# Edges of the stages in a Strassen-Winograd encoder block: five pairs begun among the token sums, separate buffers for the last down products, branch weights loaded during attention

## The chip, the cores and the metric

One core of a Trainium2 chip runs the whole block in one launch. The metric is device time in microseconds (us), the median of three runs: 2261.47 for the kernel before (2260.64 to 2265.18).

The core has a matrix engine (TensorE, PE in the rows), three elementwise engines (VectorE or DVE, ScalarE or ACT, GpSimd or POOL), and SyncE (SP), whose queue issues nearly all DMAs here. Each engine takes its instructions in the order in which they were written.

## The reference

One layer on a float32 array of 1024 tokens by 1024 features:

```python
x = x + 0.5 * swiglu(rmsnorm(x), w_gate1, w_up1, w_down1)     # FFN_DIM 2816
p = rmsnorm(x) @ w_in            # columns for attention, mLSTM and two gates
A = mla(p)                       # 8 heads, low-rank q and kv, rotary key
B = mlstm(p)                     # 4 heads, forward and backward scans
x = x + (sigmoid(g_a) * (A @ w_branch_a) + sigmoid(g_b) * (B @ w_branch_b)) @ w_out
x = x + 0.5 * swiglu(rmsnorm(x), w_gate2, w_up2, w_down2)
out = rmsnorm(x)

def swiglu(x, w_gate, w_up, w_down):
    return (jax.nn.silu(x @ w_gate) * (x @ w_up)) @ w_down
```

## The kernel before

**Numbers.** Every float32 operand of a matmul is split into a high and a low part, `H = copy to the short format` on ScalarE and `L = x - H` on VectorE. A matmul of two operands is three: HH, HL, LH. A weight quarter is split in `split_quarter` (L249 on ScalarE, L250 on VectorE), its twelve matmuls are `product` (L255 to L257), all of them from 128 rows by 512 columns.

**The large products.** Both FFNs and the output projection use a Strassen-Winograd scheme: seven products of half-size matrices stand for eight. It needs sums of quarters of the left matrix, of the right one and of the results. `combine_x` builds those of the tokens: for tiles 0 to 3 of 128 tokens it transposes, splits (L362, L363) and keeps a copy of two quarters (`kept`, copied at L369 by ScalarE); for tiles 4 to 7 it forms the sums T1 to T4 from these copies. VectorE makes most other sums (`vsum` L262, `into` L266).

**Gate and up (`gate_up`).** Column pairs j = 0 to 10, each with a gate half and an up half, each of seven products; 14 products per pair. Products 1 and 2 need only the tokens of tiles 0 to 3, so a pair can be *begun* early: `begin(j)` computes them, writes product 1 to DRAM (`f1p`) and one finished quarter to `f1h`. Pairs 0, 1 and 2 are begun, `begin(0)` before the tokens 4 to 7 are combined and the other two behind them; such a pair has ten products left in the main loop `pairs()`. The loop's step k issues product k, then prepares product k + 4 (`prep`: a sum if it needs one, ScalarE's high part, VectorE's low part right behind it), then takes in the result of product k - 1 (`post`), then one of the leftover sums of an earlier pair. `in_order` ties the engines to that order. Results go to DRAM (`f1h`, `f2h`), as do sums of the down weights (`f1w`, `f2w`). `four` in `sums_left` overwrites the tile that `two` has just stored to DRAM.

**Down (`down`).** Seven products in the order 1, 6, 2, 5, 7, 3, 4. Each runs over 11 steps j, each with two loads (L579, L580), ScalarE's high part (L582), VectorE's low part (L583) and 12 matmuls (L590). The loads take their buffers from `ring`: eight in turn, four of the pool `rw`, two with the tag `raw`, two with the tag `xn`. Where product 3 ends, the tokens 0 to 3 are final: `done` stores them and normalises them (RMS norm: L106 on ScalarE, L112 on VectorE, or L109 and L110 on GpSimd for tokens 1, 3 and 5) into tiles of the tags `xn` and `raw`, and product 4 follows, with transposes of the normalised tokens (L128) among it. In FFN1 `load_small` loads the narrow columns of `w_in` there in four pieces, again into `raw`, and splits them (L714 on ScalarE, L715 on GpSimd).

**Branch stage.** After attention, `branch_cols` loads (L1281) and splits the branch weights by column pairs; gates come from DRAM (`sg`, L1293), pass a sigmoid (L1294) and multiply the products (L1302).

Of the kernel before, what the change touches and what calls it, by code (L numbers as in the profile page):

```python
# [20 lines left out]
P = 128  # L21
# [30 lines left out]
def block_kernel(ctx, tc, a, out):  # L52
# [131 lines left out]
    QS = [P, 4, P]  # L184
# [60 lines left out]
    def split_quarter(R, src):  # L245
# [4 lines left out]
        nc.vector.tensor_tensor(out=L_, in0=src, in1=f32(H_), op=ALU.subtract)  # L250
        return H_, L_
# [17 lines left out]
    class Combined:  # L269


        def __init__(self, name, n):
            self.left = {m: [dram.tile([P, 512], F32, name=f"{name}h{m}_{j}") for j in range(n)] for m in range(1, 8)}
            self.right = {m: [dram.tile([P, 512], F32, name=f"{name}w{m}_{j}") for j in range(n)] for m in range(4, 8)}
            self.p1 = {(j, i): dram.tile([P, 512], F32, name=f"{name}p{j}_{i}") for j in range(min(n, 3)) for i in range(2)}
# [5 lines left out]
        def sums_left(self, R, j, c11, c12, c21, c22):  # L281
# [18 lines left out]
            def four():  # L300
                self.store(3, j, into(nc.vector, got[2], c21, got[2], ALU.subtract))
# [47 lines left out]
    def combine_x(R, t, xn, X, kept):  # L349
# [42 lines left out]
    AHEAD = 4  # L392

    def gate_up(R, X, wg, wu, wd, comb, hooks={}):
# [41 lines left out]
        def products_of(j, i, h):  # L436

            v = {}
# [9 lines left out]

            def prep1():
                v["w"] = {1: split_quarter(R, raws[j, i][0])}  # L450

            def prep6():
# [3 lines left out]
                v["w"] = {**v.get("w", {}), 6: split_quarter(R, v["s2"])}  # L456

            def prep2():
                v["w"][2] = split_quarter(R, raws[j, i][1])

            def prep5():
                v["w"][5] = split_quarter(R, v["s1"])

            def prep7():
                v["s3"] = vsum(R, raws[j, i][0], raws[j, i][2], ALU.subtract)
                v["w"][7] = split_quarter(R, v["s3"])

            def prep3():
                s4 = into(nc.vector, v["s2"], raws[j, i][1], v["s2"], ALU.subtract)
                v["w"][3] = split_quarter(R, s4)  # L470

            def prep4():
                v["w"][4] = split_quarter(R, raws[j, i][3])
                if i == 0 and j + 1 < n:
                    raws[j + 1, 1] = load(wu, j + 1)
                elif i == 1 and j + 1 < n:
                    ld, tails[j + 1] = comb.sums_right(wd, j + 1, R.ring)
                    ld()
                    if j + 2 < n:
                        raws[j + 2, 0] = load(wg, j + 2)  # L480

            def mm(m, bank, B, start=True):
                def f():
# [5 lines left out]
                    product(v[bank], v["w"].pop(m), X[B], start, True)  # L489
# [30 lines left out]
        def pairs():  # L520
# [8 lines left out]
            def prologue():  # L529
# [6 lines left out]
                for it in items[:AHEAD]:  # L536
                    it[1]()
# [9 lines left out]
            def step(k):  # L547
# [10 lines left out]
                del rest[:1]  # L558
            for k in range(len(items)):
# [12 lines left out]
    def down(R, comb, resid, scale, xo, done, between=lambda: None, last=3):  # L572
# [3 lines left out]
        def products(m, banks, start, stop, tails=1):  # L576
            def load(j):
                r = R.ring(2)
# [34 lines left out]

        for t in range(NT):
            nc.sync.dma_start(out=xo[t], in_=resid[t * P:(t + 1) * P, :])
        a = [R.bank(0) for _ in range(4)]
        run(1, a, True, True)
# [25 lines left out]
        run(3, c, False, True, each=c12, tails=last)  # L643
# [6 lines left out]
        run(4, e, True, True, each=c21, step=step, tails=last)  # L650
# [56 lines left out]
    def load_small(pool):  # L707
        for k in range(0, KT, 2):
            raw = raw_tile()[:, :2 * NSM].rearrange("p (k f) -> p k f", k=2)
            rows = w_in[k * P:(k + 2) * P, :].rearrange("(k p) f -> p k f", p=P)  # L710
            nc.sync.dma_start(out=raw[:, :, 0:O_M], in_=rows[:, :, 0:O_M])
            nc.sync.dma_start(out=raw[:, :, O_M:NSM], in_=rows[:, :, O_G:O_G + 16])
            wH, wL = [pool.tile([P, 2, NSM], F32R, name="ws" + n, tag=f"ws{n}{k}") for n in "HL"]
            nc.scalar.activation(out=wH, in_=raw, func=AF.Copy)  # L714
# [662 lines left out]
```

## Time and profile before

| | us |
|---|---|
| median of three runs | 2261.47 (2260.64 to 2265.18) |
| the profiled execution | 2262.68, span 2260.9 |
| TensorE busy | 2125.0 (94%) |
| VectorE busy | 1513.8 (67%) |
| ScalarE busy | 964.8 (43%) |
| GpSimd busy | 358.5 (16%) |

The mean granted clock of TensorE is 0.974 of full speed. Times of the profile are counted from the start of the span. FFN1 takes the first 720 us or so, attention ends near 1386, FFN2 begins near 1580. A duration that the profile gives for a matmul includes its way through the engine; matmuls follow each other faster than that. A row of waits says which instruction of an engine stood idle and which instruction of another released it.

### The profile page before, as it was taken

The numbers are of one execution on the slowest core, as the hardware profiler recorded it, in microseconds if no ns is written. First come the engines' busy times: TensorE is split into PE (matmuls) and PEld (weight loads), VectorE is DVE, ScalarE is ACT, GpSimd is POOL, SyncE is SP. The second block draws the span as 40 slices with busy tenths as digits, with TensorE's granted clock in tenths as the row PEclk, the third lists the DMA queues.
The fourth block names the chain that finished last, engine by engine and source line by source line (L and its number), as shares of the span: only waits on it lengthen the run. The fifth ranks groups of instructions, "written<-read, shape, count | busy, mean of one in ns | idle before, by whom it ended". The sixth has DMA issues, their size and how long they took to land.

```text
span 2260.9 us, 27801 instructions
## 1 busy us (share of the span) xinstructions
PE 2125.0 (94%) x10091; PEld 1770.4 (78%) x10091; DVE 1513.8 (67%) x2201; ACT 964.8 (43%) x1509; POOL 358.5 (16%) x307
## 2 busy tenths in 40 slices
PE   6989999999977999999999998988999999999996
PEld 4777888888856888778888887867777888888885
DVE  6777777755464666466658886567877777765564
ACT  6323333333433433544358884235623333334433
POOL 1000000000021655233445442002100000000000
PEclk9999999999988999999999999999999999999998
DMA  7554444476643433222441004875555444566643
GB/s 199 193 200 159 163 159 163 163 272 191 194 154 110 131 109 118 88 84 85 149 145 48 29 1 152 302 245 187 190 196 191 141 164 151 183 210 231 195 159 140
DMA packets 238233, 358.41 MB, mean 159 GB/s; under 512 B 23696, under 2 KB 124944, under 8 KB 238096
## 3 DMA queue, kind: packets, MB, share of 16 engines
q1 hardware_dynamic: 232912, 346.16, 46.6%
q10 hardware_dynamic: 4608, 8.39, 1.0%
q8 instruction: 79, 1.29, 0.2%
q0 software_dynamic: 576, 2.10, 0.2%
q14 instruction: 58, 0.48, 0.1%
HBM read 246.94 MB, written 109.64 MB: 158 GB/s over the span
## 4 chain that ended last, share of the span: by engine, by line
PE 73%; DVE 11%; DMA 7%; ACT 4%; issue 3%; POOL 2%; SPq 0%; DVEq 0%; ACTq 0%; POOLq 0%
PE pb L590 19%; PE pb L255 10%; PE pb L257 10%; PE pb L256 10%; PE pin L85 3%; PE pin L83 3%; PE pin L84 3%; DVE s L266 2%; PE pP L1221 2%; DMA sg<-gb_d 2%; DVE s L262 1%; PE pav L1229 1%; PE pSc L83 1%; PE pav L1230 1%; DVE w L250 1%
## 5 line engine op out<-in xcount | busy, mean ns | idle before, releaser
L590 PE MATMUL pb<-w 128*128 128x512 f32 x2184 | 505.3, 394 | 33.8 <-ACT w L582 30.4
L590 PEld LDWEIGHTS pb<-w 128*128 128x128 f32 x2184 | 414.1, 190 | 124.5 <-ACT w L582 31.9
L583 DVE TENSOR_TENSOR w<-rw,w 128x1024 fp32r<-128x1024 f32 x182 | 221.7, 1223 | 213.8 <-ACT w L582 213.8
L582 ACT ACTIVATE w<-rw 128x1024 fp32r<-128x1024 f32 x182 | 192.8, 1062 | 299.2 <-PE pb L590 269.6
L249 ACT ACTIVATE w<-s 128x512 fp32r<-128x512 f32 x176 | 109.8, 630 | 339.2 <-DVE s L262 220.9
L93 POOL TENSOR_TENSOR rs<-ms,mhalf 128x1 f32<-128x1 f32 (+3 forms) x52 | 59.8, 1151 | 971.2 <-DVE ms L98 965.0
L250 DVE TENSOR_TENSOR w<-s,w 128x512 fp32r<-128x512 f32 x176 | 121.5, 691 | 109.0 <-ACT w L249 108.8
L255 PE MATMUL pb<-XH,w 128*128 128x512 f32 x352 | 143.0, 407 | 17.3 <-ACT s L407 10.4
L83 PE MATMUL pin<-HH,dH 128*128 128x512 f32 x384 | 152.3, 397 | 0.2 <-DVE TL L1197 0.2
L85 PE MATMUL pin<-HH,dL 128*128 128x512 f32 x384 | 150.8, 394 | 0.2 <-POOL dL L159 0.2
L84 PE MATMUL pin<-HL,dH 128*128 128x512 f32 x384 | 150.9, 393 | 0.0
L255 PE MATMUL pb<-YH,w 128*128 128x512 f32 x352 | 139.6, 398 | 11.7 <-ACT s L407 7.9
L257 PE MATMUL pb<-XH,w 128*128 128x512 f32 x352 | 141.1, 401 | 2.3 <-DVE w L250 2.3
L256 PE MATMUL pb<-XL,w 128*128 128x512 f32 x352 | 141.0, 400 | 0.0
L257 PE MATMUL pb<-YH,w 128*128 128x512 f32 x352 | 138.5, 393 | 0.2 <-DVE w L250 0.2
L256 PE MATMUL pb<-YL,w 128*128 128x512 f32 x352 | 138.4, 393 | 0.0
L250 DVE TENSOR_TENSOR w<-rw,w 128x512 fp32r<-128x512 f32 x148 | 103.8, 705 | 35.6 <-ACT w L249 35.1
L249 ACT ACTIVATE w<-rw 128x512 fp32r<-128x512 f32 x148 | 91.5, 626 | 45.0 <-ACT w L249 16.0
L266 DVE TENSOR_TENSOR s<-pb,s 128x512 f32<-128x512 f32 x152 | 103.4, 685 | 7.4 <-DMA s<-f1p 2.8
L255 PEld LDWEIGHTS pb<-XH,w 128*128 128x128 f32 x352 | 68.5, 195 | 34.8 <-ACT s L407 13.0
L411 ACT ACTIVATE h<-s 128x512 f32<-128x512 f32 x66 | 41.8, 633 | 120.4 <-DVE s L266 120.4
L1001 POOL MEMSET onesg<- 64x128 f32 x1 | 0.2, 198 | 585.1 <-DVE x L612 585.1
(322 smaller groups left out, 4697.8 us busy)
## 6 DMA issues: line engine op xcount, KB each, us to landing
rw<-in_ffn_w_gate SPq DMA_DIRECT2D x50, 512.0 KB, 5.7
rw<-in_ffn_w_up SPq DMA_DIRECT2D x50, 512.0 KB, 5.1
rw<-in_ffn_w_down SPq DMA_DIRECT2D x44, 512.0 KB, 3.7
rw<-f1h SPq DMA_DIRECT2D x77, 256.0 KB, 2.7
rw<-f2h SPq DMA_DIRECT2D x77, 256.0 KB, 2.8
rw<-in_ffn_w_down SPq DMA_DIRECT2D x66, 256.0 KB, 3.0
raw<-in_w_in SPq DMA_DIRECT2D x24, 512.0 KB, 4.0
f1h<-h SPq DMA_DIRECT2D x44, 256.0 KB, 2.1
```

The source lines that it names most:

```text
L83: nc.tensor.matmul(ps, wH, mH, start=start, stop=False)
L84: nc.tensor.matmul(ps, wH, mL, start=False, stop=False)
L85: nc.tensor.matmul(ps, wL, mH, start=False, stop=stop)
L249: nc.scalar.activation(out=H_, in_=src, func=AF.Copy)
L250: nc.vector.tensor_tensor(out=L_, in0=src, in1=f32(H_), op=ALU.subtract)
L255: nc.tensor.matmul(ps, w[0][:, k, :], B[0][:, k, :], start=start and k == 0, stop=False, skip_group_check=True)
L256: nc.tensor.matmul(ps, w[0][:, k, :], B[1][:, k, :], start=False, stop=False, skip_group_check=True)
L257: nc.tensor.matmul(ps, w[1][:, k, :], B[0][:, k, :], start=False, stop=stop and k == 3, skip_group_check=True)
L266: eng.tensor_tensor(out=out, in0=a, in1=b, op=op)
L582: nc.scalar.activation(out=H_, in_=r, func=AF.Copy)
L583: nc.vector.tensor_tensor(out=L_, in0=r, in1=f32(H_), op=ALU.subtract)
L590: nc.tensor.matmul(banks[t], l[:, 0, ts_], r[:, 1, :], start=start and j == 0 and i == 0, stop=stop and j == n - 1 and i == 2, skip_group_ ...
```

## The change

- **Begun pairs.** Five pairs are begun instead of three, and `begin` now stands between the combined tokens 4 to 7.
- **Kept copies.** The copies of the two token quarters are made by GpSimd, by adding H and L, instead of by ScalarE from PSUM.
- **Order in the loop.** Step k takes in the result of product k - 1 before it prepares product k + 4, and the low part of the prepared weight stands behind the leftover sum. `four` writes into another tile.
- **Down products 3 and 4** take their load buffers from the pool `rw` alone. The loads of `x` stand behind product 1.
- **Narrow columns of `w_in`** are loaded in one piece into a tile of their own before `down` starts; their low parts move from GpSimd to VectorE. A second token tile of narrow products is computed early.
- **Branch weights** of the first column pair are loaded at step 50 of attention.

```diff
-    QS = [P, 4, P]
+    AHEAD = 4
+    BEGUN = 5
...
-                self.store(3, j, into(nc.vector, got[2], c21, got[2], ALU.subtract))
+                self.store(3, j, into(nc.vector, c21, c21, got[2], ALU.subtract))
...
-            for n, v, s in zip(("B11", "B21"), ps, kept[i]):
+            for n, v in zip(("B11", "B21"), ps):
                 put(X[n], v)
-                nc.scalar.activation(out=s, in_=v, func=AF.Copy)
+            for n, s in zip(("B11", "B21"), kept[i]):
+                nc.gpsimd.tensor_tensor(out=s, in0=f32(X[n][0][:, :, c]), in1=f32(X[n][1][:, :, c]), op=ALU.add)
...
                 mm()
-                if k + AHEAD < len(items):
-                    items[k + AHEAD][1]()
                 if k:
                     after(k - 1)
+                low = items[k + AHEAD][1]() if k + AHEAD < len(items) else None
                 for f in rest[:1]:
                     f()
                 del rest[:1]
+                if low is not None:
+                    low()
...
-        def products(m, banks, start, stop, tails=1):
+        def products(m, banks, start, stop, tails=1, raw=R.ring):
             def load(j):
-                r = R.ring(2)
+                r = raw(2)
...
-        run(3, c, False, True, each=c12, tails=last)
+        run(3, c, False, True, each=c12, tails=last, raw=R.raw)
...
-        run(4, e, True, True, each=c21, step=step, tails=last)
+        run(4, e, True, True, each=c21, step=step, tails=last, raw=R.raw)
...
-    def load_small(pool):
+    def load_small():
+        raw = big.tile([P, KT, 512], F32, name="wsr", tag="big2")[:, :, 0:NSM]
...
-            nc.gpsimd.tensor_tensor(out=wL, in0=raw, in1=f32(wH), op=ALU.subtract)
+            nc.vector.tensor_tensor(out=wL, in0=raw[:, k:k + 2, :], in1=f32(wH), op=ALU.subtract)
...
         for t in range(4, NT):
+            begin(t - 3)
             combine_x(R, t, xn.pop(t), X, kept)
-        begin(1)
-        begin(2)
...
+            if s == 50:
+                for n in ("w_branch_b", "w_branch_a"):
+                    branch_ahead[n] = raw_tile().rearrange("p (k f) -> p k f", k=4)
```

Three places where instructions stand in another order. First SyncE's queue where product 3 of FFN1's down stage passes into product 4: `f1h_0_141` to `f1h_3_144` are the left quarters of product 4's steps 0 to 3, `x_d` the stores of the final tokens, `in_w_in` the narrow columns. Before:

```order
L770 DMA x_d<-x_3905 128x1024
L579 DMA rw<-f1h_2_143 128x512
L580 DMA rw<-f1w_2_187 128x512
L579 DMA rw<-f1h_3_144 128x512
L580 DMA rw<-f1w_3_188 128x512
L711 DMA raw<-in_w_in 128x2x416
L712 DMA raw<-in_w_in 128x2x16
...
L579 DMA rw<-f1h_0_141 128x512
L580 DMA rw<-f1w_0_185 128x512
```

Now:

```order
L591 DMA rw<-f1h_0_141 128x512
L592 DMA rw<-f1w_0_185 128x512
L591 DMA rw<-f1h_1_142 128x512
L592 DMA rw<-f1w_1_186 128x512
L591 DMA rw<-f1h_2_143 128x512
L592 DMA rw<-f1w_2_187 128x512
...
L786 DMA x_d<-x_3930 128x1024
```

The loads of steps 0 and 1 stood behind the stores and behind four pairs of loads of `w_in`; now the steps stand in their order, ahead of the stores, and `w_in` is no longer among them.

Second, VectorE in the main loop, in a begun pair of FFN1: `s<-rw` are the two sums of a product to be prepared, `w` its low part, `s<-pb` the intake of a result. Before:

```order
L266 TENSOR_TENSOR rw_960<-rw_960 128x512
L262 TENSOR_TENSOR s_1090<-rw_849,rw_850 128x512
L262 TENSOR_TENSOR s_1092<-s_1090,rw_849 128x512
L250 TENSOR_TENSOR w_1094<-s_1092,w_1094 128x512
L266 TENSOR_TENSOR s_1052<-pb_1051,s_1052 128x512
L266 TENSOR_TENSOR rw_960<-rw_962,rw_960 128x512
```

Now, the same step:

```order
L271 TENSOR_TENSOR s_1443<-pb_1442,s_1443 128x512
L267 TENSOR_TENSOR s_1482<-rw_1229,rw_1230 128x512
L267 TENSOR_TENSOR s_1484<-s_1482,rw_1229 128x512
L271 TENSOR_TENSOR rw_1350<-rw_1352,rw_1350 128x512
L251 TENSOR_TENSOR w_1486<-s_1484,w_1486 128x512
```

The intake moved ahead of the sums, and the leftover sum stands between the second sum and the low part that needs ScalarE's high part of it.

Third, SyncE's queue at the end of attention: `tok` are attention's own loads, `x` the tokens for the next stage. Before:

```order
L1177 DMA tok_10937<-qk_d 128x8x192
L1177 DMA tok_10939<-qk_d 128x8x192
L615 DMA x_12871<-x_d 128x1024
L615 DMA x_12872<-x_d 128x1024
L615 DMA x_12873<-x_d 128x1024
L615 DMA x_12874<-x_d 128x1024
L1281 DMA rw<-in_w_branch_b 128x4x256
L1281 DMA rw<-in_w_branch_a 128x4x256
```

Now:

```order
L1293 DMA raw<-in_w_branch_b 128x4x256
L1193 DMA tok_10956<-qk_d 128x8x192
L1193 DMA tok_10958<-qk_d 128x8x192
L1293 DMA raw<-in_w_branch_a 128x4x256
L629 DMA x_12896<-x_d 128x1024
```

The branch weights moved ahead of the four loads of `x`.

## Rows read from the trace of the kernel before

**Rows 1.** The page's span and its part 1, busy time of each engine.

```profile
span 2260.9 us, 27801 instructions
PE 2125.0 (94%) x10091; PEld 1770.4 (78%) x10091; DVE 1513.8 (67%) x2201; ACT 964.8 (43%) x1509; POOL 358.5 (16%) x307
```

**Rows 2.** Busy time by stretch, with granted clock (PEclk) and DMA, in us.

```profile
core 0: us, PE busy (x) PEld busy (x) DVE busy (x) ACT busy (x) POOL busy (x), PEclk, DMA share, GB/s
30.00:60.00 30.00, 23.73 (x102) 19.01 (x101) 25.76 (x43) 19.69 (x35) 1.22 (x18) 0.84 0.51 157
90.00:180.00 90.00, 79.54 (x329) 63.57 (x328) 68.63 (x108) 25.36 (x44) 0.00 (x0) 0.95 0.55 189
650.00:730.00 80.00, 51.40 (x220) 41.63 (x219) 37.43 (x44) 31.51 (x45) 25.62 (x18) 0.79 0.39 133
1380.00:1400.00 20.00, 10.15 (x53) 8.57 (x54) 8.47 (x15) 6.32 (x13) 2.19 (x3) 0.74 0.69 235
1570.00:1640.00 70.00, 59.07 (x267) 47.37 (x266) 61.57 (x95) 43.65 (x80) 19.01 (x14) 0.90 0.62 210
1690.00:1730.00 40.00, 32.13 (x128) 25.34 (x127) 30.96 (x50) 10.78 (x19) 0.00 (x0) 0.91 0.52 178
2210.00:2250.00 40.00, 29.99 (x125) 24.08 (x123) 18.31 (x22) 13.03 (x19) 3.07 (x4) 0.87 0.36 125
200.00:440.00 240.00, 240.00 (x1060) 198.75 (x1059) 179.63 (x278) 80.78 (x137) 0.00 (x0) 1.00 0.47 159
```

**Rows 3.** TensorE's waits, 30 to 180 us: waiter, releaser, total, times, longest.

```profile
PE pb L255 <- ACT s L407: 10.4, 5, 4.7
```

**Rows 4.** VectorE's waits, 76 to 180 us.

```profile
DVE w L250 <- ACT w L249: 16.6, 22, 1.2
DVE s L266 <- DMA f1h<-s: 5.7, 2, 3.4
```

**Rows 5.** Timeline, 649 to 720 us: start, duration, engine, line, tiles [idle before <-releaser].

```profile
649.83 7.42 PE L590 MATMUL pb<-w 128*128 128x512 f32 x32
668.06 0.38 SPq L711 DMA_DIRECT2D raw<-in_w_in  x1
681.68 0.34 SPq L579 DMA_DIRECT2D rw<-f1h  x1
686.22 33.11 PE L590 MATMUL pb<-w 128*128 128x512 f32 x132 [15.62 <-ACT w L582]
```

**Rows 6.** Timeline at the end of attention, 1382 to 1396 us.

```profile
1382.20 5.40 SPq L615 DMA_DIRECT2D x<-x_d  x4
1387.71 0.38 SPq L1281 DMA_DIRECT2D rw<-in_w_branch_b  x1
1387.18 0.41 ACT L1236 ACTIVATE aH<-lo 64x256 fp32r<-64x256 f32 x1 [0.48 <-DVE lo L1235]
1395.34 0.80 PE L83 MATMUL pb<-bH,w 128*128 128x512 f32 x1 [9.12 <-ACT w L249]
```

**Rows 7.** Waits and timeline on GpSimd and VectorE, 1570 to 1640 us.

```profile
PE pb L358 <- POOL xn L110: 3.4, 1, 3.4
1573.96 3.20 POOL L110 TENSOR_TENSOR xn<-xn,nw 128x1024 f32<-128x1024 f32 x1
1579.93 2.36 POOL L110 TENSOR_TENSOR raw<-raw,nw 128x1024 f32<-128x1024 f32 x1
1575.47 2.24 DVE L250 TENSOR_TENSOR w<-rw,w 128x512 fp32r<-128x512 f32 x1
1578.24 0.70 DVE L250 TENSOR_TENSOR w<-rw,w 128x512 fp32r<-128x512 f32 x1
```

**Rows 8.** TensorE's waits, 1690 to 1730 us.

```profile
PE pb L255 <- ACT s L407: 7.9, 3, 4.5
```

**Rows 9.** Timeline of the last product, 2187 to 2250 us.

```profile
2223.30 0.44 SPq L580 DMA_DIRECT2D rw<-f2w  x1
2228.42 20.89 PE L590 MATMUL pb<-w 128*128 128x512 f32 x84 [9.32 <-ACT w L582]
```

More of the change, by code (lines that the diff above doesn't have):

```diff
@@ L249, in split_quarter @@
         nc.scalar.activation(out=H_, in_=src, func=AF.Copy)
-        nc.vector.tensor_tensor(out=L_, in0=src, in1=f32(H_), op=ALU.subtract)
-        return H_, L_
+        return (H_, L_), lambda: nc.vector.tensor_tensor(out=L_, in0=src, in1=f32(H_), op=ALU.subtract)
+    def split_quarter(R, src):
+        w, low = high_quarter(R, src)
+        low()
+        return w
     def product(ps, w, B, start, stop):
@@ L436, in products_of @@
         def products_of(j, i, h):
-            v = {}
+            v, w = {}, {}
             def act(key, val, psum=None):
@@ L447, in act, with high @@
                         comb.store(key, j, h[key])
+            def high(m, s):
+                w[m], low = high_quarter(R, s)
+                return low
             def prep1():
-                v["w"] = {1: split_quarter(R, raws[j, i][0])}
+                return high(1, raws[j, i][0])
             def prep6():
@@ L455, in prep6, with rest @@
                 v["s2"] = vsum(R, v["s1"], a11, ALU.subtract)
-                v["w"] = {**v.get("w", {}), 6: split_quarter(R, v["s2"])}
+                return high(6, v["s2"])
             def prep2():
-                v["w"][2] = split_quarter(R, raws[j, i][1])
+                return high(2, raws[j, i][1])
             def prep5():
-                v["w"][5] = split_quarter(R, v["s1"])
+                return high(5, v["s1"])
             def prep7():
-                v["s3"] = vsum(R, raws[j, i][0], raws[j, i][2], ALU.subtract)
-                v["w"][7] = split_quarter(R, v["s3"])
+                return high(7, vsum(R, raws[j, i][0], raws[j, i][2], ALU.subtract))
             def prep3():
-                s4 = into(nc.vector, v["s2"], raws[j, i][1], v["s2"], ALU.subtract)
-                v["w"][3] = split_quarter(R, s4)
+                return high(3, into(nc.vector, v["s2"], raws[j, i][1], v["s2"], ALU.subtract))
             def prep4():
[L473 to L480, printed above, removed]
+                low = high(4, raws[j, i][3])
+                def rest():
+                    low()
+                    if i == 0 and j + 1 < n:
+                        raws[j + 1, 1] = load(wu, j + 1)
+                    elif i == 1 and j + 1 < n:
+                        ld, tails[j + 1] = comb.sums_right(wd, j + 1, R.ring)
+                        ld()
+                        if j + 2 < n:
+                            raws[j + 2, 0] = load(wg, j + 2)
+                return rest
             def mm(m, bank, B, start=True):
@@ L488, in f @@
                         nc.sync.dma_start(out=v["p1"], in_=saved[j][i])
-                    product(v[bank], v["w"].pop(m), X[B], start, True)
+                    product(v[bank], w.pop(m), X[B], start, True)
                 return f
@@ L1237, in weigh, with gate_rows @@
             nc.gpsimd.tensor_tensor(out=aL[r, h // 2, cq], in0=lo[r], in1=f32(aH[r, h // 2, cq]), op=ALU.subtract)
+        branch_ahead, gates_ahead = {}, []
+        def gate_rows(src, fs):
+            g = nscr.tile([P, S], F32, name="sg", tag="xn")
+            nc.sync.dma_start(out=g, in_=src[fs, :])
+            return g
         load_pair(0)
@@ L1291, in block_kernel @@
                 for src in (gb_d, ga_d):
-                    g = nscr.tile([P, S], F32, name="sg", tag="xn")
-                    nc.sync.dma_start(out=g, in_=src[fs, :])
+                    g = gates_ahead.pop(0) if gates_ahead else gate_rows(src, fs)
                     nc.scalar.activation(out=g, in_=g, func=AF.Sigmoid)
```

48 lines of the change are left out of this document (27 added, 21 removed).

## The prediction

> **What bounds the kernel now.** I read part 1 of the page first: TensorE is busy for 2125.0 of 2260.9 us [rows 1]. The change adds no matmul, so what it can win lies in the 136 us in which TensorE stands idle, and in the slower clock granted around them. I then asked for busy time by stretch [rows 2]. In the middle of the pair loop, 200 to 440 us, TensorE has no idle time, the clock is 1.00, and 1060 matmuls take 240 us, 0.226 us each, so a product of twelve takes 2.72 us; VectorE is busy for 75% there (179.63 of 240). Nothing is to be won in such a stretch. Seven others show idle time: 6.3 us in 30 to 60, 10.5 in 90 to 180, 28.6 in 650 to 730, 9.9 in 1380 to 1400, 10.9 in 1570 to 1640, 7.9 in 1690 to 1730 and 10.0 in 2210 to 2250. Together that is 84 us, over half of all idle time, and every edit but one (the loads of x) lies in one of them. The waits and the timeline of each then say who is late.
>
> **The change part by part.** The sum is made against the profiled execution, 2262.68 us, which is 1.8 longer than its span and 1.2 over the median.
>
> *Down product 3 to 4 of FFN1.* Product 3 ends at 657.25 (649.83 + 7.42), product 4 runs from 686.22 to 719.33 without a break [rows 5]. Between them TensorE only transposes tokens 0 to 3, and its last wait there is 15.62 us for ScalarE's split of the first step. That split waits for a load which SyncE issues at 681.68, behind the loads of w_in that began at 668.06: both use the buffers tagged raw, which the normalised tokens hold as well. Now steps 0 to 5 are loaded in rw ahead of the stores, and product 4's matmuls stand in front of the transposes and among them. Of the 62.1 us from 657.25 on, 132 matmuls at 0.226 are 29.9. In 650 to 730 TensorE is busy for 51.40, of which 7.25 belong to product 3 and 33.11 to product 4; of the other 11.0, transposes on both sides of product 4, I count half, 5.5. That leaves 62.1 - 29.9 - 5.5 = 26.7. I take 24, since the transposes among the matmuls still depend on GpSimd's norms. Bounds: 12 (a new wait half as long as the old one takes its place) to 27. The low parts of w_in move to VectorE, which is busy for 37.43 of the 80 us, so four more instructions cost nothing.
>
> *End of FFN2.* Here too the load for product 4's step 4 is issued only at 2223.30, behind stores of the output in a raw buffer, and TensorE waits 9.32 us; the 84 matmuls left take 20.89 instead of 19.0 [rows 9], because the granted clock is down (mean 0.87 in 2210 to 2250 [rows 2]). With rw alone only the order of the steps is left: 9.3 + 1.9 = 11.2, of which I take 10. Bounds 8 and 11. The last 12 us (from 2249.3), final norm and output, are untouched.
>
> *Attention to branch.* The loads of the branch weights are issued at 1387.71, behind four loads of x that occupy the queue from 1382.20 for 5.40 us; the first matmul starts at 1395.34 after 9.12 us [rows 6]. With the weights there, ScalarE can split once its last piece of attention is written, at 1387.59, and one split takes about 0.6 (the 0.70 of VectorE's partner is the nearest row [rows 7]), so TensorE starts near 1388.3: 7 us. Bounds: 5 to 9 (with the clock, 0.74 in these 20 us). Ahead of the moved loads nothing else waits on SyncE but two of attention's own loads.
>
> *Begun pairs in FFN1.* In 90 to 180 TensorE loses 10.5 us though VectorE has the load of the undisturbed stretch (68.63 of 90, 76%), so it is order and not throughput. TensorE's waits, 10.4 us, are for ScalarE's copy of a result, L407 [rows 3], which stands behind the high part of a weight whose sum VectorE has not made yet. VectorE itself waits 16.6 us in 22 pieces for ScalarE's high part, because the low part follows right behind the sum, and 5.7 us for a store, because `four` overwrites what is being stored [rows 4]. All three orders are changed: intake first, low part last, another tile. I take 9 of 10.5; bounds 3 and 14 (with the clock, 0.95). Two more begun pairs move four products each from the loop to the front, and add ten loads (four of half weights, four of product 1, two of f1h) and four stores for each FFN, to a queue that is half busy there (DMA share 0.55).
>
> *Token sums, 30 to 60 us.* 6.3 us idle, VectorE busy for 25.76 of 30: here VectorE is the bound. With begin(1) to begin(4) between the sums TensorE has 4 x 4 x 2.72 = 43.5 us of matmuls to cover them. I take 5; bounds 0 and 8.
>
> *Begun pairs in FFN2.* Same loop, 7.9 us idle for the same copy [rows 8]: I take 7, bounds 2 and 10.
>
> *Edge to FFN2.* 10.9 us idle in 1570 to 1640, the longest wait 3.4 us for GpSimd's norm [rows 7]. ScalarE loses eight copies, GpSimd gains eight additions of 128 by 512; by half of the 2.36 us for 128 by 1024 that is about 1.2 each, 9.4 together, on an engine that is busy for 19.01 of the 70 us. It also meets VectorE: a low part of 0.70 us took 2.24 while GpSimd's L110 ran from 1573.96 for 3.20 [rows 7]; it ended 0.55 us behind it. So each addition may cost VectorE up to its own length, in a stretch where VectorE is busy for 61.57 of 70. Against that stand begin(0) to begin(3) among the sums, 10.9 us of matmuls each. I take a gain of 2; bounds -10 and 5.
>
> The Trainium skill states this as a rule (page "SBUF — State Buffer", section "SBUF: two separate sides"): VectorE with two operands in SBUF and GpSimd share a pair of ports, held for a whole instruction, while the other is blocked. The trace agrees, with the 2.24 us above; by the rule the moved copies cost VectorE up to 9.4 us for each FFN, and the sum would be 19 us smaller if VectorE set the pace in both; by the busy shares above it does not.
>
> For what I did not find, above all GpSimd's additions in FFN1 and the longer list of DMAs, I take off 2 (0 to 10).
>
> Sum: 24 + 10 + 7 + 9 + 5 + 7 + 2 - 2 = 62. 2262.7 - 62 = 2200.7; in the median, 1.2 less, 2199.5, say 2200. All lower bounds together give 12 + 8 + 5 + 3 + 0 + 2 - 10 - 10 = 10, or 2251; all upper ones 27 + 11 + 9 + 14 + 8 + 10 + 5 = 84, or 2177.
>
> **The rivals.**
>
> *The begun stages stay as they are.* Ten products take 27.2 us, and five such pairs follow each other, so VectorE, already 76% busy, gets no rest between them; new waits replace the old. Then only the two product edges and the branch weights pay: 24 + 10 + 7 = 41, so 2220. For it: VectorE is at 61.57 of 70 in the FFN2 edge. Against it: 75% in the undisturbed loop costs nothing.
>
> *GpSimd's additions block VectorE* in both token stages, as reckoned: 19 us less, 2219. For it: the 2.24 us row; against it: 43.5 us of matmuls that cover them.
>
> *The new wait at the FFN1 edge.* Tokens 1 and 3 are normalised on GpSimd, 2.36 us for L110 alone, and a transpose in front of matmuls stops them all. If half of the 24 us comes back as waits on GpSimd, 2212.
>
> *Slower: the deferred low parts.* The low part now stands behind the intake and the leftover sum. If VectorE falls so far behind that a low part is written after TensorE wants it, every product of both loops pays. A quarter of a microsecond in each of 2 x 11 x 14 = 308 products is 77 us, and the time would be 2262 + 77 - 62 = 2277. It decides from a lag of four products, 10.9 us, since weights are prepared four ahead; VectorE's 75% says it has 0.7 us to spare in each 2.72.
>
> **How the numbers follow.** The forecast as worked out 0.55; begun stages unchanged 0.18; GpSimd against VectorE 0.08; the wait at the FFN1 edge 0.12; slower 0.05; the rest, 0.02, no change, where gains and new waits cancel. Between 2184 and 2234 lie the first four, apart from their tails. About 0.2%, 4.5 us, is what a measurement of this kernel can tell from none: faster 0.93, same 0.02, slower 0.05.
>
> **What would show it.** Product 4 of FFN1 should start within 3 us of 657 and no wait above 3 us should stand in the transposes; the first branch matmul 2 us behind attention's last; no wait of L590 near the end; fewer than 3 us of waits for the copy L407 (now L412) in the begun pairs; VectorE's waits for ScalarE's high part well under 16.6. The forecast is wrong if TensorE's idle time stays above 90 us, or if waits for GpSimd take the place of those for ScalarE.

## The result and the profile after

The changed kernel takes 2183.59 us (2182.63 to 2187.11) against 2261.57: a ratio of 0.9655 [0.9638, 0.9672], 78 us faster. The forecast was 2200, with a range of 2184 to 2234, so the time lies just outside it: the direction and most stages came out as argued, the sum was 16 us short.

The page's span and part 1 of the changed kernel; they answer to [rows 1]:

```profile
span 2182.1 us, 27814 instructions
PE 2107.3 (97%) x10091; PEld 1761.1 (81%) x10091; DVE 1520.4 (70%) x2205; ACT 954.6 (44%) x1493; POOL 376.5 (17%) x319
```

The span fell by 78.8 us. TensorE's idle time, span less busy, fell from 135.9 to 74.8, which is 61.1. The other 17.7 us came off its busy time, 2125.0 to 2107.3, with the same 10091 matmuls. To see where, both executions are cut at the same events: the first and the last matmul of gate and up in each FFN, the first product of the input projection, the last of attention, the first of the branch stage, the first transpose of FFN2, the end. Columns as in [rows 2]; the first numbers are the cut, its length, and TensorE's busy time. The kernel before:

```profile
0.00:20.55 20.55, 7.76 (x32) 6.19 (x33) 11.35 (x19) 14.23 (x26) 2.94 (x11) 1.00 0.91 256
20.55:476.33 455.78, 436.18 (x1882) 357.33 (x1880) 339.34 (x537) 162.50 (x278) 3.71 (x20) 0.98 0.53 175
476.33:743.62 267.29, 235.49 (x1042) 194.70 (x1040) 142.50 (x154) 107.76 (x127) 31.22 (x24) 0.94 0.54 175
743.62:1386.22 642.60, 628.37 (x3587) 542.15 (x3585) 431.75 (x661) 355.51 (x610) 295.08 (x230) 0.99 0.27 86
1386.22:1395.34 9.12, 0.00 (x1) 0.00 (x1) 0.44 (x2) 1.48 (x4) 0.72 (x1) 0.63 0.90 303
1395.34:1572.82 177.48, 169.57 (x720) 137.49 (x721) 115.09 (x164) 63.67 (x78) 3.38 (x4) 0.97 0.73 248
1572.82:2027.30 454.48, 435.69 (x1913) 358.04 (x1911) 346.62 (x534) 169.03 (x290) 16.19 (x11) 0.98 0.53 179
2027.30:2260.90 233.60, 211.99 (x926) 174.49 (x924) 126.71 (x133) 90.62 (x98) 5.23 (x8) 0.96 0.56 184
```

The changed kernel:

```profile
0.00:24.45 24.45, 7.82 (x33) 6.28 (x33) 15.72 (x20) 13.94 (x25) 10.88 (x16) 1.00 0.89 249
24.45:460.39 435.94, 429.15 (x1880) 353.18 (x1881) 338.73 (x536) 158.33 (x272) 7.55 (x24) 0.99 0.58 192
460.39:704.46 244.07, 232.84 (x1042) 193.44 (x1040) 147.38 (x163) 106.16 (x130) 23.83 (x20) 0.97 0.58 191
704.46:1343.98 639.52, 627.35 (x3587) 540.96 (x3585) 425.21 (x657) 355.87 (x607) 296.39 (x229) 1.00 0.28 89
1343.98:1346.06 2.08, 0.00 (x1) 0.00 (x0) 0.43 (x2) 1.47 (x4) 0.62 (x1) 1.00 0.44 96
1346.06:1521.48 175.42, 167.41 (x721) 136.86 (x721) 118.75 (x164) 64.19 (x78) 5.92 (x6) 0.98 0.77 265
1521.48:1959.65 438.17, 432.60 (x1911) 356.98 (x1912) 347.66 (x535) 163.99 (x282) 25.26 (x17) 0.99 0.58 194
1959.65:2182.10 222.45, 210.12 (x926) 173.36 (x924) 126.55 (x133) 90.62 (x98) 6.08 (x8) 0.98 0.58 193
```

Row by row, the change in length, and the part of it that is idle time and busy time:

| stage | forecast | length | idle | busy |
|---|---|---|---|---|
| to the first product | | +3.9 | +3.8 | +0.1 |
| FFN1 gate and up | -14 | -19.8 | -12.8 | -7.0 |
| FFN1 down and its edges | -24 | -23.2 | -20.6 | -2.7 |
| projection, mLSTM, attention | | -3.1 | -2.1 | -1.0 |
| attention to branch | -7 | -7.0 | -7.0 | 0 |
| branch and output projection | | -2.1 | +0.1 | -2.2 |
| FFN2 edge, gate and up | -9 | -16.3 | -13.2 | -3.1 |
| FFN2 down and output | -10 | -11.2 | -9.3 | -1.9 |
| reserve | +2 | | | |

Two stages without a forecast, together 5.2 us, can't be put down to an edit: in the kernels below that change nothing in them, the one with projection and attention takes 638.1 to 642.5 us, the branch stage 170.7 to 177.8.

The waits that were to go have gone. The token sums first: 30 to 60 us of the changed kernel, where TensorE was busy for 23.73 us at a clock of 0.84 [rows 2]:

```profile
30.00:60.00 30.00, 30.00 (x142) 24.89 (x141) 18.75 (x28) 16.91 (x30) 2.15 (x4) 1.00 0.75 230
```

TensorE's waits in 76 to 180 us, against [rows 3]:

```profile
PE pb L261 <- DVE T2L L368: 3.4, 1, 3.4
PE pb L260 <- ACT T2H L367: 2.4, 1, 2.4
PE pb L260 <- ACT h L430: 0.3, 1, 0.3
PE pb L260 <- ACT s L412: 0.3, 1, 0.3
```

10.4 us for the copy of a result (L407, now L412) have become 0.3. What is left is a token sum, T2, that comes late. With the pairs behind the sums (u_fivelate, below) no wait for it stands there; with the position constants built earlier (i_kept_const) 1.9 and 1.9 us of it remain. In FFN2 the 7.9 us for the copies [rows 8] have gone too; all of TensorE's waits in 1560 to 1960 us are:

```profile
PE pb L260 <- ACT s L412: 0.7, 3, 0.2
```

VectorE in 76 to 180 us, against [rows 4]: its wait for ScalarE's high part is 10.5 instead of 16.6, and the wait for the store is not there.

```profile
DVE w L251 <- ACT w L250: 10.5, 22, 1.2
```

TensorE at the FFN1 edge, against [rows 5]: product 3 runs straight into product 4, the transposes of tokens 0 to 3 stand among its matmuls, and one wait of 2.01 is left there. The last line is behind product 4: for tokens 4 and on the wait of 3.32 that stood there before (3.32 too) has stayed, so the sign "no wait above 3 us in the transposes" holds for tokens 0 to 3 only.

```profile
627.80 22.60 PE L602 MATMUL pb<-w 128*128 128x512 f32 x99
650.24 1.03 PE L128 MATMUL psT<-ident,xn 128*128 128x128 f32 x8
651.03 2.58 PE L602 MATMUL pb<-w 128*128 128x512 f32 x10
...
663.30 3.15 PE L602 MATMUL pb<-w 128*128 128x512 f32 x8 [2.01 <-DVE w L595]
...
682.14 1.94 PE L128 MATMUL psT<-ident,xn 128*128 128x128 f32 x8 [3.32 <-DVE ms L98]
```

The first branch product, against [rows 6], waits 2.08 instead of 9.12:

```profile
1346.06 0.50 PE L83 MATMUL pb<-bH,w 128*128 128x512 f32 x1 [2.08 <-ACT w L250]
```

And from 1970 us to the end of the products, against the 9.32 of [rows 9], all of TensorE's waits are:

```profile
PE pb L602 <- DVE w L595: 0.7, 1, 0.7
```

### The profile page after: what moved, and what is told of

It is laid out like the page before. It is cut to its first block, busy times and chain, and to the rows that moved or that the text cites. A ratio compares the mean times of both kernels' runs of the same rounds, so it can differ in the third digit from the quotient of the medians.

```text
span 2182.1 us, 27814 instructions
## 1 busy us (share of the span) xinstructions
PE 2107.3 (97%) x10091; PEld 1761.1 (81%) x10091; DVE 1520.4 (70%) x2205; ACT 954.6 (44%) x1493; POOL 376.5 (17%) x319
## 3 DMA queue, kind: packets, MB, share of 16 engines
q8 instruction: 79, 1.29, 0.2%
## 4 chain that ended last, share of the span: by engine, by line
PE 42%; DVE 8%; ACT 3%; issue 2%; DMA 2%; POOL 2%; DVEq 0%; SPq 0%; ACTq 0%; POOLq 0%
PE pb L602 11%; PE pb L261 5%; PE pb L262 5%; PE pb L260 5%; PE pP L1237 2%; PE pav L1245 1%; PE pSc L83 1%; PE pav L1246 1%; DVE s L271 1%; PE pSc L84 1%; PE pSc L85 1%; PE pb L83 1%; PE pb L84 1%; PE pb L85 1%; DVE w L251 1%
## 5 line engine op out<-in xcount | busy, mean ns | idle before, releaser
L602 PEld LDWEIGHTS pb<-w 128*128 128x128 f32 x2184 | 410.8, 189 | 95.7 <-DVE w L595 10.3
L93 POOL TENSOR_TENSOR rs<-ms,mhalf 128x1 f32<-128x1 f32 (+3 forms) x52 | 61.8, 1193 | 1019.5 <-DVE ms L98 1012.8
L260 PE MATMUL pb<-XH,w 128*128 128x512 f32 x352 | 138.9, 397 | 2.3 <-ACT XH L367 1.3
L262 PE MATMUL pb<-XH,w 128*128 128x512 f32 x352 | 137.0, 391 | 0.0
L1229 POOL TENSOR_SCALAR pe<-pe,ri 128x1024 f32<-128x1024 f32 x64 | 72.0, 1126 | 112.1 <-DVE ri L1228 106.5
L1239 DVE TENSOR_TENSOR PL<-pP,PH 128x512 fp32r<-128x512 f32 x128 | 82.9, 679 | 7.2 <-ACT PH L1238 7.2
## 6 DMA issues: line engine op xcount, KB each, us to landing
rw<-f1h SPq DMA_DIRECT2D x77, 256.0 KB, 2.8
rw<-f2h SPq DMA_DIRECT2D x77, 256.0 KB, 2.7
rw<-in_ffn_w_down SPq DMA_DIRECT2D x66, 256.0 KB, 3.0
f1h<-h SPq DMA_DIRECT2D x55, 256.0 KB, 2.4
f2h<-h SPq DMA_DIRECT2D x55, 256.0 KB, 2.3
```

Source lines behind the costliest of these rows:

```text
L260: nc.tensor.matmul(ps, w[0][:, k, :], B[0][:, k, :], start=start and k == 0, stop=False, skip_group_check=True)
L262: nc.tensor.matmul(ps, w[1][:, k, :], B[0][:, k, :], start=False, stop=stop and k == 3, skip_group_check=True)
L602: nc.tensor.matmul(banks[t], l[:, 0, ts_], r[:, 1, :], start=start and j == 0 and i == 0, stop=stop and j == n - 1 and i == 2, skip_group_ ...
```

## The experiments

The question is why the sum was short: by time at the lower clock that it did not count, or by an edit worth more than its stretch. Most kernels undo a part of the change. The kernel before ran beside each of them, with medians between 2259.5 and 2265.7; a ratio is to the one that ran beside.

| kernel | us | ratio to before, 95% interval |
|---|---|---|
| changed, second time (again) | 2182.16 | 0.9645 [0.9616, 0.9674] |
| three begun pairs (u_three) | 2199.70 | 0.9716 [0.9688, 0.9744] |
| five, but behind the sums (u_fivelate) | 2195.42 | 0.9687 [0.967, 0.9704] |
| old order (u_order) | 2199.25 | 0.9717 [0.9699, 0.9736] |
| old tile for the stored sum (u_four) | 2181.33 | 0.9641 [0.9613, 0.9668] |
| old order, old tile (u_order_four) | 2230.45 | 0.9845 [0.9822, 0.9868] |
| three pairs, old order (u_three_order) | 2205.95 | 0.9751 [0.9723, 0.9779] |
| before + five pairs (b_five) | 2283.98 | 1.0082 [1.0063, 1.0101] |
| before + new order and tile (b_order) | 2239.52 | 0.9878 [0.9858, 0.9898] |
| ring of eight for products 3, 4 (u_ring) | 2207.62 | 0.9755 [0.974, 0.977] |
| w_in in four pieces (u_small) | 2178.08 | 0.9628 [0.9597, 0.9659] |
| both (u_ring_small) | 2214.67 | 0.9785 [0.9755, 0.9814] |
| late branch weights (u_branch) | 2186.25 | 0.966 [0.9626, 0.9693] |
| copies by ScalarE (u_kept) | 2178.97 | 0.9626 [0.9606, 0.9646] |
| copies by ScalarE, early constants (i_kept_const) | 2178.34 | 0.9621 [0.9599, 0.9643] |
| copies by ScalarE, w_in in pieces (i_kept_small) | 2180.76 | 0.9626 [0.9606, 0.9646] |
| one gap, 30 copies (c_gap30) | 2197.64 | 0.9711 [0.9681, 0.974] |
| one gap, 45 copies (c_gap45) | 2208.48 | 0.9755 [0.9721, 0.979] |

**How far one build moves.** 

> The changed kernel itself, beside these. It says how far one build moves between chips and executions: 2183.6 within 3 us, and by stage within 2 us, if the differences of 2 to 5 us between the runs so far are real; more than that, and they are not to be told apart.

It held for the whole, 2182.16, and nearly by stage: none of the table differs by more than 2.3 us from the first execution. TensorE's busy time over the whole span differs by 3.1 (2104.2 against 2107.3). Differences of under 4 us between these kernels are therefore not told apart.

**What an idle stretch costs.**

```diff
             def high(m, s):
                 w[m], low = high_quarter(R, s)
+                if gap and (j, i, m) == (8, 0, 6):
+                    for _ in range(gap):
+                        nc.scalar.activation(out=w[m][0], in_=s, func=AF.Copy)
```

> The changed kernel with 30 more ScalarE copies of the same high part, at one place in the quiet middle of FFN1's pair loop (pair 8). At 0.52 us each they hold ScalarE for 15.6 us; four products, 10.9 us, are prepared ahead, so TensorE should stand idle once for about 5 us. Theory 1 (an idle stretch costs its length and then busy time at the lower clock): idle time of the first gate and up stage up by 5, its busy time up by 1 to 3, whole 2190. Theory 2 (the clock follows idle time only by its own length, busy time stays): busy time of the stage within 0.5 us of 429.

> The same with 45 copies, 23.4 us, so one idle stretch of about 12.5 us. Theory 1: idle up by 12.5 and busy time up by 3 to 5, 2200. Theory 2: 2196, busy time as it was. If the loss of clock belongs to the wait and not to its length, the busy time grows as much as with 30 copies.

FFN1's gate and up stage of the changed kernel run again, then of the kernel with 30 copies, then with 45:

```profile
24.28:459.36 435.08, 428.55 (x1879) 352.87 (x1880) 338.80 (x536) 158.19 (x272) 7.64 (x24) 0.99 0.59 193
```

```profile
24.41:476.20 451.79, 432.57 (x1879) 354.93 (x1880) 338.29 (x536) 176.85 (x302) 7.59 (x24) 0.97 0.57 185
```

```profile
24.28:488.53 464.25, 433.99 (x1879) 356.14 (x1880) 338.56 (x536) 186.36 (x317) 7.68 (x24) 0.96 0.55 180
```

TensorE's waits around the gap, with 30 copies and with 45:

```profile
PE pb L260 <- ACT w L462: 10.3, 1, 10.3
PE pb L260 <- ACT s L416: 3.0, 1, 3.0
```

```profile
PE pb L260 <- ACT w L462: 20.2, 1, 20.2
PE pb L260 <- ACT s L416: 3.4, 1, 3.4
```

The stage's busy time grows by 4.0 us (432.57 less 428.55) for 13.3 us of waits and by 5.4 for 23.6. So theory 1 holds: an idle stretch costs its length and then busy time at the lower clock, though more of it than the 1 to 3 us and 3 to 5 us expected. The rows behind the gap with 30 copies show where:

```profile
358.00:362.00 4.00, 4.00 (x11) 3.08 (x10) 3.90 (x8) 0.40 (x1) 0.00 (x0) 0.50 0.18 66
366.00:366.80 0.80, 0.80 (x4) 0.67 (x5) 0.80 (x3) 0.12 (x1) 0.00 (x0) 1.00 0.87 328
367.40:370.00 2.60, 2.60 (x8) 2.02 (x7) 2.60 (x5) 0.43 (x1) 0.00 (x0) 0.50 0.58 163
372.00:382.00 10.00, 10.00 (x46) 8.27 (x45) 7.61 (x13) 3.42 (x6) 0.00 (x0) 1.00 0.51 179
```

Behind the wait of 10.3 us the next product runs at 0.50, the lower of the two levels of the clock, in the timeline a matmul every 0.43 us instead of 0.23. After the wait of 3.0 us a few matmuls follow at full clock, then it falls to 0.50 once more, until near 370.4. So the 4.0 and the 5.4 us are each the price of two waits together; a price for one wait can't be read from them, only that nearly twice the idle time added 1.4 us. The gaps came out longer than expected, because a copy behind another took 0.66 us (45 of them 29.75 in the timeline) and not 0.52.

The traces also show that it is the clock by which busy times differ. Take each stretch of TensorE's busy time times the share of the clock that was not granted in it, and add up: 32.3 us in the kernel before, 18.5 and 14.2 in the two executions of the changed kernel. That is 13.8 of the 17.7 us. What remains of the busy time is 2092.8, 2088.8 and 2090.1; over all twenty traces it stays between 2087.8 and 2092.8, while the busy time itself goes from 2103.4 to 2130.2.

**Number of pairs, order and tile.** The old order prepares the low part before the intake; the old tile:

```diff
-                self.store(3, j, into(nc.vector, c21, c21, got[2], ALU.subtract))
+                self.store(3, j, into(nc.vector, got[2], c21, got[2], ALU.subtract))
```

and three pairs:

```diff
-    BEGUN = 5
+    BEGUN = 3
...
         for t in range(4, NT):
-            begin(t - 3)
             combine_x(R, t, xn.pop(t), X, kept)
+        begin(1)
+        begin(2)
```

> The changed kernel (2183.6 us) with three begun pairs, standing where they stood before; all else as changed. The forecast missed 16 us. Theory 1: the missing part is time that TensorE spends busy at the lower clock around each idle stretch, which the forecast counted only where a whole stretch was taken; then every edit that is undone costs its idle time and about 0.3 us of busy time more for each idle us. Here 7 us of idle time come back (30 to 60 us, and the edge to FFN2) and 3 us of clock: 2194, TensorE's busy time up by about 3 from 2107.3. Theory 2: one edit was worth far more than its stretch; if it is the begun pairs, 16 us and more come back, 2200 or over. If the loop's order does all the work, 2186 or less.

> The changed kernel with the old order of the loop's step (preparation with its low part first, then the intake, then the leftover sum); five pairs begun. Theory 1: the waits for the copy of a result come back in ten begun pairs instead of six, 10.4 + 7.9 us of idle time by the rows of before, about 18, and 5 us of clock: 2206, TensorE's busy time up by 5. Theory 2 (the order is not what counts, the store that four overwrote is): under 2188.

> The changed kernel (2183.6 us) with three begun pairs in their old places and the old order of the loop's step. Undone alone, the first cost 16.1 us and the second 15.7. Theory 1 (each part removes stalls of its own, so the two add): 32 more, 2215. Theory 2 (they work on the same stalls: the new order matters because five pairs are begun, or the other way about): 2200 to 2206. With both undone the two gate and up stages should stand near the kernel before: 456 and 454 us.

> The changed kernel with the fourth leftover sum written over the tile that has just been stored, as before. Before, VectorE waited 3.4 and 2.3 us for that store in the first begun pairs. If that stall was part of what held up the results' copies: 5 to 10 us slower, 2189 to 2194. If the low parts behind the leftover sum leave room for it: within 2 us of 2183.6.

Each alone costs 16 us, both 22 to 24 instead of 32, the tile nothing. 2206 is the upper end of what the third text's second theory gave: number and order share stalls of 8 to 10 us.

The first two texts also ask for the clock. In the two gate and up stages, cut as above, idle time rises against the changed kernel by 12.4 us with three pairs, 13.6 with the old order and 16.8 with both, and busy time by 5.1, 3.1 and 7.4. With three pairs that is more idle time than the 7 us of theory 1. The 0.3 us of busy time for each idle us is of the right size (here 0.2 to 0.4), but no constant. The gate and up stages with both undone are 448 and 451 us long and not 456 and 454 as expected. The two kernels built on the kernel before, and the last one, show what is missing.

> The kernel before (2261.5 us) with only the new order of the loop's step and the fourth leftover sum into another tile. In the changed kernel the order was worth 6.3 us with three begun pairs and 15.7 with five; the store's part, which vanished with five, showed as about 4 us of waits for the copies in each FFN in the old order. Expected here: 6 for the order and 6 for the tile with their clock, 2249. If order and number only work together: 2258.

> The kernel before with only five begun pairs among the token sums; old order, old tile. With the new tile five pairs were worth 6.7 us at the old order. Two more begun pairs also bring two more stalls on the store (2.3 to 3.4 us of VectorE each). Expected: 2257, gate and up stages 452 and 451 us long; if the stalls eat it up, 2262 or more, and then the number alone is worth nothing.

> The changed kernel with the old order of the loop's step and the fourth leftover sum written over the tile just stored. On the kernel before, five begun pairs alone made it 20 us slower, with VectorE waiting 14.3 and 11.3 us for that store; in the changed kernel the old tile alone cost nothing and the old order alone 15.7 us. If the store's stall needs the old order to reach TensorE: 25 us over the old order alone, 2224, waits for the copies of results near 18 us in FFN1's first 300 us and VectorE's waits for the store above 10. If the other edits have removed it: 2200.

Five pairs make the kernel before slower, by 0.8% [0.6, 1.0]; order and tile make it 1.2% [1.0, 1.4] faster, 26 us where I expected 12. Both kernels keep two edits of the change that lie outside of gate and up: the later loads of x, and the loads of the first two gate tiles, which the change also moves to step 50 of attention. So the stages are the better measure: gate and up take 462.3 and 467.7 us with five pairs and 447.3 and 443.9 with order and tile, against 455.8 and 454.5. That is 19.7 us longer and 19.1 shorter.

VectorE's wait for the store, 60 to 300 us, in before + five pairs:

```profile
DVE s L271 <- DMA f1h<-s: 14.3, 4, 4.5
```

TensorE's largest wait there in total, 18 to 300 us:

```profile
PE pb L260 <- ACT s L411: 18.6, 5, 5.5
```

and VectorE's in the changed kernel with old order and old tile:

```profile
DVE s L271 <- DMA f1h<-s: 13.2, 4, 4.0
```

In the kernel before the store cost VectorE 5.7 us in two waits [rows 4]; with five pairs it is four waits, 14.3 us. In the old order a VectorE that waits for the store holds up the next preparation, ScalarE's high part behind that, and the copy of a result behind that, for which TensorE waits. With five pairs, old order and new tile 2199, with new order and old tile 2181, with both old 2230, 6 more than expected. Between 60 and 300 us VectorE waits for the store in neither of the first two, and TensorE's waits for the copies, 18 to 300 us, are 8.3, 0.7 and 14.7 in these three. So either repair takes the store's stall away, and five pairs pay only with one of them. The new order takes more than the store's stall: with the new tile it is worth 16 to 17 us at five pairs and 6 at three. The order is two edits, the intake ahead of the preparation and the low part behind the leftover sum; no kernel has one without the other.

> The changed kernel with five begun pairs, but pairs 1 to 4 (in FFN2 also the first stands as before) behind the combined tokens instead of among them. If the place among the sums is what counts in the token stage, the waits of three begun pairs for the token sums come back (2.5, 2.1 and 2.3 us at 46 to 58 us, with clock some 10 us) in FFN1 and about as much in FFN2: 2198. If only the number counts: within 3 us of 2183.

It came to 2195.42, between the two. Against the second execution of the changed kernel FFN1's gate and up stage ends 1.9 us later and FFN2's is 7.6 longer; with three pairs it was 9.1 and 7.5. So in FFN2 the place among the sums is what counts, in FFN1 mostly the number.

**The FFN1 edge.**

```diff
-        run(3, c, False, True, each=c12, tails=last, raw=R.raw)
+        run(3, c, False, True, each=c12, tails=last)
...
-        wsraw = load_small()
...
-            split_small(smallp.enter_context(spool(name="ws", bufs=1, side="right")), wsraw)
+            load_small(smallp.enter_context(spool(name="ws", bufs=1, side="right")))
```

> The changed kernel with down products 3 and 4 on the ring of eight buffers again; the narrow columns stay in one load. Theory 1: at the end of FFN2 9 us of idle time and 2 of clock come back; at the FFN1 edge the loads of steps 0 and 1 again wait for the normalised tokens, but no longer for w_in: 8 us idle and 4 of clock. Together 23, 2207. Theory 2 (the load of w_in was the whole matter in FFN1): only the end comes back, 2195.

> The changed kernel with the narrow columns of w_in loaded in four pieces at the edge of product 3 and 4, and split with GpSimd, as before; the down loads stay in their own buffers. Theory 1 (the down loads waited because they shared buffers and the queue): the four loads and GpSimd's four splits delay only the normalised tokens and the early narrow products, 2 to 5 us, 2186 to 2189. Rival (the load of w_in at that place was the matter): 12 us or more, 2196.

> The changed kernel with both edits at FFN1's edge undone: the ring of eight buffers for products 3 and 4, and the narrow columns in four pieces there. The ring alone cost 24 us, 11.9 of them in FFN1's down stage and 12.8 at the end; the four pieces alone cost nothing. Theory: with the shared buffers the four pieces stand in the way, with separate ones they don't, so together FFN1's down stage gives back what the change won there, 23 us (267 us long instead of 244), and the whole is 2219. Rival (the pieces are harmless in either case): 2207, as with the ring alone.

FFN1's down stage is 244 us long as changed, 243.7 with the pieces alone, 256.0 with the ring alone and 267.2 with both, as before (267.3); the whole with both is 2214.67 and not 2219. TensorE's wait for the first split of product 4 is 15.0 us with both (620 to 760 us):

```profile
PE pb L602 <- ACT w L594: 15.0, 1, 15.0
```

With the ring alone it is 0.6 there; the time is lost in the transposes, which then stand together again:

```profile
PE psT L128 <- DVE ms L98: 6.6, 2, 3.3
PE psT L128 <- POOL xn L110: 3.7, 2, 1.8
PE psT L128 <- POOL raw L110: 2.4, 1, 2.4
```

The ring costs what theory 1 said, 24 us: 8.9 us of idle time and 3.1 of busy time in FFN1's down stage, 10.0 and 2.8 at the end, where the one long wait is 9.9 again. But in FFN1 theory 1 named the wrong wait: the first split comes in time, the norms don't. What puts the transposes together again is not shown. The pieces cost less than it said; their 2178.08 is lower than the changed kernel, with intervals that overlap. So separate buffers are sufficient, and the single load of w_in adds nothing to them; it helps only with the ring.

**Branch weights.**

```diff
-                for n in ("w_branch_b", "w_branch_a"):
-                    branch_ahead[n] = raw_tile().rearrange("p (k f) -> p k f", k=4)
-                    nc.sync.dma_start(out=branch_ahead[n], in_=a[n][0][:, 0:256].rearrange("(k p) f -> p k f", p=P))
```

> The changed kernel without the early load of the branch weights. The gap between attention and branch was 9.1 us and is 2.1. Theory 1: 7 us of idle time and 1 of clock, 2191.5. Rival (the branch stage is paced by the loads of the gates, so what is won is waited for later): within 3 us.

TensorE's wait at that place is 8.5 us again, but the whole is only 3 to 4 us slower, at the edge of what can be told. By stage the rival doesn't show: from the end of attention to the first transpose of FFN2 it takes 183.0 us, against 177.5 and 175.2 in the two executions of the changed kernel. But the branch stage alone varies by 7 us between kernels that leave it as it is, so whether part of the 7 us is lost again is not settled.

**Copies on GpSimd, and versions meant to be faster.**

```diff
-                nc.gpsimd.tensor_tensor(out=s, in0=f32(X[n][0][:, :, c]), in1=f32(X[n][1][:, :, c]), op=ALU.add)
+                nc.scalar.activation(out=s, in_=v, func=AF.Copy)
```

> The changed kernel with the kept copies made by ScalarE from PSUM as before. Theory 1: neither engine is the bound in the token sums, so within 2 us of 2183.6. Rival (GpSimd's additions hold VectorE's two-operand instructions up): 4 to 10 us faster, 2174 to 2180, and VectorE's L112 of 3.4 us near 1520 and 1545 back to 1.3. Other rival (ScalarE was late before, as the 2.7 us wait for its copies said): 3 to 6 us slower.

> A version meant to beat the changed kernel (2182 to 2184 us): the kept copies by ScalarE again (with them the first gate and up product starts at 20.1 us instead of 24.4), and the position constants, which stand on VectorE behind the token sums where TensorE now waits 3.4 and 2.4 us for T2, built ahead of the begun pairs 1 to 4, where VectorE is only 60% busy. If GpSimd's additions and the constants are what is late: 4 us at the start, 6 us idle and 3 of clock, 2171. If the constants then delay the sums of tokens 4 to 7 instead: 2179, as with the copies alone.

> A version meant to beat the changed kernel: kept copies by ScalarE again and the narrow columns in four pieces at the edge, the two undone edits whose runs came out at 2179 and 2178. If both were gains: 2174. If they were within what executions differ by: 2178 to 2183. By stage the copies should give 4 us at the start and the rest nothing.

With ScalarE's copies the first product starts at 20.1 us, as before, instead of 24.4; FFN1's first stage ends 2 to 3 us earlier in one of these kernels and 0.3 later in the other. With the constants moved ahead the start was at 24.3 again. The L112 of 3.4 us near 1520 and 1545, which the first text puts down to the additions, run beside GpSimd's norms (L110); beside the additions L112 takes 2.27 and 2.31. With ScalarE's copies three of the five L112 there take 1.28 or 1.29, and the two beside the first norm still 2.15 and 3.31. The three lie at 2178 to 2181 against 2182 and 2184, their intervals overlap, and none is shown to beat the changed kernel.

Not undone by themselves, and so without a price of their own: the later loads of x, the early loads of two gate tiles, and the second early tile of narrow products.

## Why the prediction was wrong

- **The step that failed is the term for the clock in the sum.** I took idle time stretch by stretch and put the clock into the upper bounds ("bounds 3 and 14 (with the clock, 0.95)"), except where a whole product was replaced: 3.2 us at the FFN1 edge (33.11 less 29.9) and 1.9 at the end, 5.1 in all. The runs show 17.7 us off TensorE's busy time, 13.8 of them by the granted clock alone, and the gap kernels show that idle stretches bring it about: 4.0 and 5.4 us for two waits each. Idle time itself fell by 61.1, where the sum without its clock terms had 57, so the way from idle stretch to gain was right. With 17.7 in place of 5.1 the forecast would have been 2187, 3 us from the measured time. The rows for it stood in [rows 2]: mean granted clocks of 0.74 to 0.95 over the seven stretches, whose busy time times the share not granted is 34 us. Taken in the proportion of the idle time that the sum wins there (57 of 84) it is 23, an estimate after the fact, and the forecast 2182. My own upper bounds came to 2177; the range stopped at 2184 all the same.
- **Edge to FFN2 and its begun pairs: 9 forecast, 16.3 measured**, of which 13.2 are idle time. I had bounded the edge at -10 for GpSimd's additions. They do hold VectorE up (beside them L112 takes 2.27 us at 1532 and 2.31 at 1538), but no cost to this stage can be told: with ScalarE's copies it is 437.7 us long, against 438.2 and 439.8. What counts is that the begun pairs stand among the sums: placed behind them, the stage is 7.6 us longer.
- **Begun pairs and token sums of FFN1: 14 forecast, 19.8 less 3.9 at the start measured.** The mechanism was the one named, intake and copies behind VectorE; 7.0 of the 19.8 are busy time. But the parts do not add as I listed them: five pairs in the kernel before are a loss of some 20 us in the two FFNs, and order or tile turns it into a gain.
- **The FFN1 edge: 24 forecast, 23.2 measured, with one remedy more than it took.** The wait of 15.62 has the two causes that I named, the shared buffers and the loads of w_in: it is back, at 15.0, only with both undone. But separate buffers alone take it away, and with them the loads of w_in don't matter.
- **Attention to branch (7, 7.0) and the end (10, 11.2)** came out as worked out, each as a stretch; the first is only partly confirmed in the whole. The 11.2 at the end are 9.3 of idle time and 1.9 of clock, as worked out; I had taken 10 of them.
- **The reserve for GpSimd's additions in FFN1** sat at a real place, though not the one I had looked at: 3.9 us before the first product.
- **The rivals.** The slower one, late low parts, did not happen. Its point of decision, a lag of 10.9 us, was near the mark for ScalarE's high parts at least: in the gap kernels ScalarE was held for about 19.8 and 29.7 us (30 and 45 copies of 0.66) and TensorE waited 10.3 and 20.2 us, a slack of 9.5. The way to a slower kernel that is real here, the store's stall repeated in five pairs, I had in [rows 4] and used only as a gain.

## What to carry to other kernels

Price an idle stretch of TensorE at its length plus the busy time that runs at the lower clock around it. The kernels here gave 0.2 to 0.5 us of busy time for each idle us (0.5 in the stages of u_order_four), so take it from the rows of the stretch itself, busy time times the share of the clock not granted, and check the sum against span less busy. Before repeating a piece of work that shows a stall, ask whether the stall repeats with it: a buffer overwritten while its store is under way cost two waits with three pairs and four with five. Edits on the same chain of engines don't add; undo them one by one and in pairs.

## What the runs showed of the hardware

GpSimd and VectorE hold each other up from the first microseconds on. Timeline of GpSimd in the changed kernel, then of VectorE:

```profile
13.02 0.55 POOL L93 TENSOR_TENSOR rs<-ms,mhalf 128x1 f32<-128x1 f32 x1
13.54 1.27 POOL L375 TENSOR_TENSOR s<-XH,XL 128x512 f32<-128x512 f32 x1
14.76 1.53 POOL L93 TENSOR_TENSOR rs<-ms,mhalf 128x1 f32<-128x1 f32 x1
```

```profile
13.61 2.28 DVE L112 SCALAR_TENSOR_TENSOR raw<-x,rs,nw 128x1024 f32<-128x1024 f32 x1
19.76 1.27 DVE L112 SCALAR_TENSOR_TENSOR raw<-x,rs,nw 128x1024 f32<-128x1024 f32 x1
```

The same VectorE instruction takes 2.28 us when it starts just behind GpSimd's addition of two tiles and 1.27 alone; the addition ends at 14.81, and 2.28 less the 1.20 until then is 1.08. GpSimd's L93, which then meets the rest of L112, takes 1.53 us instead of 0.55. This agrees with the rule of the Trainium skill (page "SBUF — State Buffer", section "SBUF: two separate sides") that one of the two is blocked for the length of the other's instruction. It costs time where VectorE sets the pace, as at the start. There TensorE waits for the delayed instruction (0 to 25 us):

```profile
PE pb L363 <- DVE raw L112: 6.1, 2, 3.2
```

With ScalarE's copies no wait for it stands there, and the first product starts 4 us earlier. In the edge to FFN2 no cost can be told: 437.7 us with ScalarE's copies, 438.2 and 439.8 without.
